# The low parts of the last MLP's weights, made by a transfer that adds

## The chip, the cores and the metric

The kernel runs on one core of one Trainium2 chip. The metric is device time in microseconds for one launch, from the first to the last instruction of the program with what lies around it. Several runs are given with their median.

## The reference

Two transformer blocks on 512 tokens of 1024 features, in float32. The first block has two softmax attentions, gates and an MLP; the second has two layers, each a mixer followed by an MLP with a squared ReLU. Only the last of these MLPs is touched:

```
def _sqrelu_mlp(h, w1, w2):                       # h 512 x 1024, w1 1024 x 4096, w2 4096 x 1024
    return jnp.square(jax.nn.relu(h @ w1)) @ w2

    # second_block, layer 1
    h = _rmsnorm(x, mlp_norm_g[layer])
    x = x + _sqrelu_mlp(h, mlp_w1[layer], mlp_w2[layer])
```

## The kernel before

TensorE takes its operands in a rounded form of float32 (F32R, "fp32r" in the profile). To keep the accuracy of float32, every operand is split into a high part h, the rounded value, and a low part l, the rest: a product is three matmuls, high by high, high by low and low by high, summed in one PSUM bank (`mm3`).

Activations lie with features on partitions, as eight tiles [128, 512 tokens], split into aH and aL. Weights come from DRAM in blocks of [128, 1024], 512 KB each. `load_w` fetches one (tile wraw, four buffers, by SP's queue), ScalarE copies it into the rounded tile wH (three buffers), and VectorE subtracts: wL = wraw - wH (three buffers). In some earlier stages GpSimd does the subtraction (`pool_l`, `lean`); in the layer in question it is VectorE for every block.

`gemm_t_steps` makes one output tile [128, 512] from one block: eight steps of three matmuls, 24 in all. The first `group` tiles of a call go side by side: for each step k the matmuls of tile 0 and tile 1, and those of tile 2 three steps later (`lag`). From then on a tile follows a tile. There are three accumulators in PSUM.

`mlp` goes over the 4096 hidden features in four chunks of 1024. In each chunk the first product makes eight hidden tiles (Relu by ScalarE, times itself by VectorE, split into the pair hd), and the second product takes these through eight blocks of w2; its results are scaled and added to X (`upd`: VectorE multiplies, GpSimd adds, VectorE in the last chunk). That is 64 weight blocks in all. The call of the last layer has `group=3`, which bears on the first chunk only, and its last output tile goes by halves of the tokens, so that its end is short.

The last layer is called at the end of `block_two`, straight after the output product of the odd mixer (`od_out`, eight tiles, line 870), whose results are added to X, squared for the row mean, and split as H by `split_gain` (lines 341 and 342).

The program is laid out by a scheduler at build time, which gives each engine its order from the dependences, the order of the program and its own estimate of when things are ready. At run time every engine, and each queue, works through its instructions in that order.

Of the kernel before, what the change touches and what calls it, by code (L numbers as in the profile page):

```python
# [14 lines left out]
AF = mybir.ActivationFunctionType  # L15
OP = mybir.AluOpType
# [4 lines left out]
P = 128  # L21
# [30 lines left out]
class Weave:  # L52
    """Places small dependent work on TensorE among the steps of long matrix products.

    A task is a generator: it emits one stage, then yields the TensorE time (us, estimated)
    before which its next stage should not stand in TensorE's queue, or a function that
    gives that time, or None while it isn't known."""

# [56 lines left out]
class Build:  # L115
    def __init__(self, nc, tc, ctx, a, out, dbg=None):
        self.nc, self.tc, self.a, self.out, self.dbg = nc, tc, a, out, dbg
        self.ctx = ctx
        self.weave = Weave(self)
        self.lean = False  # L120
        pool = lambda **k: ctx.enter_context(tc.tile_pool(**k))
        self.cn = pool(name="cn", bufs=1)
        self.xp = pool(name="xp", bufs=1)
        self.ap = pool(name="ap", bufs=1)
        self.wp = pool(name="wp", bufs=1)
        self.sm = pool(name="sm", bufs=1)
        self.ps = pool(name="ps", bufs=1, space=PSUM)
        self.dr = pool(name="dr", bufs=1, space=DRAM)
# [49 lines left out]
    def load_w(self, src, n=1024, pools=None, pool_h=False, pool_l=False):  # L178
        nc = self.nc
        (hp, hn, hb), (lp, ln, lb) = pools or ((self.wp, "wH", 3), (self.wp, "wL", 3))  # L180
        r = self.wp.tile([P, 1024], F32, name="wraw", bufs=4)
        nc.sync.dma_start(r[:, :n], src)
        h = hp.tile([P, 1024], F32R, name=hn, bufs=hb)
        if pool_h:
            nc.gpsimd.tensor_scalar(h[:, :n], r[:, :n], 1.0, 0.0, op0=OP.mult, op1=OP.add)
        else:
            nc.scalar.activation(h[:, :n], r[:, :n], AF.Copy)  # L187
        l = lp.tile([P, 1024], F32R, name=ln, bufs=lb)
        (nc.gpsimd if pool_l else nc.vector).tensor_tensor(l[:, :n], r[:, :n], h[:, :n], op=OP.subtract)  # L189
        return h, l  # L190
# [21 lines left out]
    def gemm_t_steps(self, srcs, xs, evac, group=1, kt=KT, pool_l=(), ks=None, halves=False, last=None):  # L212
        """out^T tile m = W[:, 128 m:]^T x^T; srcs: one block [128, kt*128] per tile.

        halves: the first group goes over one half of the tokens first; last: evacuates the
        last tile instead of evac, half by half."""
        m = 0
# [28 lines left out]
    def gemm_n_steps(self, srcs, xs, evac):  # L246
        """out tile [128 tokens, 512] = x W; srcs: four blocks [128, 2 k tiles, 512]."""
        accs = [self.acc() for _ in range(3)] + [self.pg()]
# [24 lines left out]
    def rsqrt(self, out, a, eps):  # L273
        """out = (a + eps) ** -0.5 by Newton steps; small tiles, a may lie in PSUM."""
        nc = self.nc
# [12 lines left out]
    def sumsq(self, src, k, tag="ssq", scale=1.0, apart=False):  # L288
        """adds the squares of tile k (features on partitions) to a running tile, or returns them."""
        nc = self.nc  # L290
        if k == 0:
            s = self.sm.tile([P, NT], F32, name=tag, bufs=1)
            nc.scalar.activation(s, src, AF.Square, scale=scale)
            self.cur[tag] = s
        else:
            q = self.sm.tile([P, NT], F32, name="sq", bufs=2)
            nc.scalar.activation(q, src, AF.Square, scale=scale)
            if apart:
                return q
            nc.vector.tensor_tensor(self.cur[tag], self.cur[tag], q, op=OP.add)  # L300

    def mean_rows(self, *parts, pool=None):
        """mean over features as PSUM [128, 512], the same in every partition."""
        ps = (pool or self.pg)()
# [4 lines left out]
    def rstd_rows(self, ms, name="R"):  # L309
        """(ms + eps) ** -0.5 as SBUF [128, 512]."""  # L310
        nc = self.nc
# [5 lines left out]
    def cols_of(self, R, pool=None):  # L317
        """[128 tokens, 4] columns of rows that are the same in every partition."""
        nc = self.nc
# [7 lines left out]
    def modulate(self, x, k, R, A, shift, hl=None, c=slice(0, NT)):  # L327
        """x R A + shift of tile k, split."""
        nc = self.nc
# [25 lines left out]
def block_one(B):  # L355
    nc, tc, a = B.nc, B.tc, B.a
    with ExitStack() as st:
# [25 lines left out]
        def ada_first(c):  # L383
            """128 columns of shift1 and of scale1, four row tiles at a time side by side on TensorE."""
            pa = B.pmisc()
# [15 lines left out]
        def ada_vec(c):  # L401
            """the same columns on VectorE."""
            row = at.tile([P, 512], F32, name="ada", bufs=2)
# [7 lines left out]
        def ada(part, cb):  # L411
            """512 columns of the modulation, on VectorE."""
            ac = at.tile([P, 512], F32, name="ada", bufs=2)
# [40 lines left out]
        def ev_q(tiles, acc):  # L454
            """1/8 of two heads of 64 rows, each block of 128 queries back to front: for each head
            a tile with the high part in the head's own rows and the low part in the other ones."""
            for b, t in enumerate(tiles):
# [7 lines left out]
        def ev_k(tiles, acc):  # L465
            """for each of two heads a tile with the high part twice; the low parts of both in a third one."""
            for b, t in enumerate(tiles[:2]):
# [67 lines left out]
        def ev_g(m, acc):  # L535
            """sigmoid as exp(-ln(1 + exp(-x)))."""
            t = at.tile([P, NT], F32, name="gt", bufs=4)
# [42 lines left out]
        def ev_last(c, acc):  # L580
            """the last tile of the residual, by halves."""
            t = X[7] if c.start else load_x(7)
# [80 lines left out]
def flip_blocks(t):  # L663
    """columns of [128, 512] with each block of 128 back to front."""
    return bass.AP(tensor=t.tensor, offset=t.offset + P - 1, ap=[t.ap[0], [P, 4], [-1, P]])


def load_strips(B, at):
    """bucket of each distance as one-hot columns with the mask's rows, and the heads' biases."""
    nc, a = B.nc, B.a  # L670
# [7 lines left out]
def bias_strips(B, at, oh):  # L678
    """masked bias by reversed distance, one row per head, in DRAM."""
    nc = B.nc  # L680
# [9 lines left out]
def bias_tile(B, at, h, off, n):  # L690
    """[128 queries, n] additive bias of head h, already masked; the last query first."""
    t = B.strip
# [6 lines left out]
class Attention:  # L699
    """the two softmax attentions of block one, as tasks; heads share buffers, counted in free."""  # L700

# [17 lines left out]
    def head(self, key, h, b, q, k, strip, spans, qk_banks, pt_banks, times, sink=None):  # L719
        """P^T of one head; spans: first and last key of each query tile; banks: tiles that share a PSUM bank."""  # L720
        B, at, W, free = self.B, self.at, self.W, self.free
# [106 lines left out]
def mlp(B, hp, w1, w2, H, upd, group=1, pool_l=(), during=None, mid=None, last=None):  # L828
    """during: called with each step's number in the first product, which goes over half of the tokens first; mid: called after it."""
    nc = B.nc  # L830
# [43 lines left out]
def sq_mlp(B, layer):  # L874
    nc, tc, a, X = B.nc, B.tc, B.a, B.X
    with ExitStack() as st:
# [19 lines left out]
        def end(c, acc):  # L896
            t = hp.tile([P, NT], F32, name="up", bufs=3)[:, c]
            nc.vector.tensor_tensor(t, acc[:, c], R2[:, c], op=OP.mult)
            nc.vector.tensor_tensor(X[7][:, c], X[7][:, c], t, op=OP.add)
            nc.sync.dma_start(B.out[:, 7, c], X[7][:, c])  # L900
        mlp(B, hp, a[f"mlp1_{layer}"], a[f"mlp2_{layer}"], H, upd, group=3, mid=norm, last=end if layer else None)


def even_mixer(B, ev, H):
# [11 lines left out]
    def stats():  # L916
        """rstd of both norms, and the end of the first one."""
        l1 = B.sm.tile([P, NT], F32, name="sq", bufs=2)
# [55 lines left out]
    def gelu(t):  # L974
        """t <- gelu(t), tanh form: t * exp(-ln(1 + exp(-2 u)))."""
        g = ev.tile([P, NT], F32, name="ge", bufs=3)
# [84 lines left out]
    def stick_head(j, b, As):  # L1061
        """A^T of one head, key tiles side by side, masked."""
        need = ("qk", 2 * j), ("qk", 2 * j + 1)
# [26 lines left out]
    def split_y():  # L1090
        """parts of the result take the place of H once that is used up."""
        for k in range(KT):
# [36 lines left out]
def stick_scores(B, ev, q, k, z, h, l, tiles):  # L1129
    """masked scores of some key tiles, and log(1 + exp) of them in two parts."""  # L1130
    nc = B.nc
# [21 lines left out]
def stick_weights(B, z, h, l, tiles):  # L1153
    """z <- exp(z - the sum over this key and the later ones), for some key tiles."""
    nc = B.nc
# [284 lines left out]
```

## Time and profile before

| what | value |
|---|---|
| median of 3 runs | 1937.0 us (1934.53 to 1937.11) |
| span of the profiled execution | 1936.0 us, 1.0 us under the median |
| busy PE / VectorE / ScalarE / GpSimd | 98% / 55% / 40% / 11% of the span |
| DRAM read | 193.86 MB |
| mean DMA rate | 102 GB/s |

The profiled execution is one run; its own time is known by its span. PE is TensorE's matmul queue and PEld its weight loads, which run beside the matmuls; DVE is VectorE, ACT ScalarE, POOL GpSimd, SP the engine that issues the loads. A matmul's shown length contains its pipeline, so that successive matmuls overlap in the rows; the distance from start to start is what counts. Idle time of an engine that is not on the chain which ended last costs nothing.

### The profile page before, as it was taken

How to read it: one execution, taken by the hardware profiler on the slowest of the kernel's cores; microseconds unless marked ns; L12 is line 12 of the kernel's file. 1: busy time of each engine (PE TensorE's matmuls, PEld its weight loads, DVE VectorE, ACT ScalarE, POOL GpSimd, SP SyncE). 2: the span in 40 equal slices, each digit the busy share in tenths (PEclk: the TensorE clock that was granted, in tenths of full speed). 3: DMA queues.
4: the chain of work that ended last, by engine and by line, in shares of the span. 5: the costliest groups of instructions: out<-in, count | busy, mean ns of one | idle time of the engine just before them, and what ended most of it. 6: DMA issues, size and time to landing. Idle time of an engine off the chain costs nothing.

```text
span 1936.0 us, 22136 instructions
## 1 busy us (share of the span) xinstructions
PE 1898.4 (98%) x8570; PEld 1501.6 (78%) x8570; DVE 1066.2 (55%) x1571; ACT 767.3 (40%) x1246; POOL 212.5 (11%) x149
## 2 busy tenths in 40 slices
PE   6999999999999999999899999999999999999999
PEld 3777778888888887776688888888777888888887
DVE  4765668664434346667755445546745554454544
ACT  2455454342323244666634232233436343223231
POOL 1000010010000001325320201100201001210100
PEclk8999999999999999999999999999999999999999
DMA  6523258522223223211122322222231233223221
GB/s 233 165 55 104 89 170 261 188 88 89 97 98 98 89 96 115 66 55 55 44 88 98 98 92 96 96 98 90 89 108 44 77 101 106 97 89 98 98 98 66
DMA packets 61640, 197.43 MB, mean 102 GB/s; under 512 B 6904, under 2 KB 8490, under 8 KB 61536
## 3 DMA queue, kind: packets, MB, share of 16 engines
q1 hardware_dynamic: 57864, 190.34, 29.8%
q10 hardware_dynamic: 3672, 5.69, 1.1%
q8 instruction: 67, 1.10, 0.2%
q14 instruction: 37, 0.30, 0.1%
HBM read 193.86 MB, written 2.15 MB: 101 GB/s over the span
## 4 chain that ended last, share of the span: by engine, by line
PE 88%; DVE 7%; ACT 3%; issue 1%; DMA 1%; SPq 0%; DVEq 0%; ACTq 0%
PE acc L193 79%; PE pm L193 5%; PE pg L193 2%; PE po L193 1%; DVE s L1230 1%; DVE sl L1150 1%; PE pm L196 1%; DMA oh<-ada 1%; ACT wH L187 0%; DVE wL L189 0%; ACT sz L1168 0%; ACT se L1146 0%; ACT se L1147 0%; DVE ge L979 0%; DVE aL L335 0%
## 5 line engine op out<-in xcount | busy, mean ns | idle before, releaser
L187 ACT ACTIVATE wH<-wraw 128x1024 fp32r<-128x1024 f32 (+1 forms) x304 | 314.7, 1037 | 752.3 <-PE acc L193 683.0
L189 DVE TENSOR_TENSOR wL<-wraw,wH 128x1024 fp32r<-128x1024 f32 (+1 forms) x269 | 365.1, 1358 | 298.9 <-ACT wH L187 291.9
L193 PE MATMUL acc<-aH,wH 128*128 128x512 f32 (+1 forms) x1296 | 507.3, 392 | 5.5 <-ACT aH L334 5.0
L193 PE MATMUL acc<-aL,wH 128*128 128x512 f32 (+1 forms) x1296 | 502.2, 387 | 3.4 <-DVE aL L335 3.4
L193 PE MATMUL acc<-aH,wL 128*128 128x512 f32 (+1 forms) x1296 | 501.5, 387 | 0.0
L193 PE MATMUL acc<-hd,wH 128*128 128x512 f32 (+1 forms) x1552 | 483.2, 392 | 0.0
L193 PEld LDWEIGHTS acc<-hd,wH 128*128 128x128 f32 x1552 | 289.4, 187 | 70.8 <-issue 1.0
L193 PE MATMUL acc<-hd,wL 128*128 128x512 f32 (+1 forms) x776 | 304.0, 392 | 0.0
L193 PEld LDWEIGHTS acc<-aH,wH 128*128 128x128 f32 x1296 | 244.2, 189 | 62.7 <-issue 9.2
L193 PEld LDWEIGHTS acc<-aL,wH 128*128 128x128 f32 x1296 | 244.4, 189 | 53.8 <-DVE aL L335 4.3
L193 PEld LDWEIGHTS acc<-aH,wL 128*128 128x128 f32 x1296 | 244.4, 189 | 50.7 <-issue 1.2
L193 PEld LDWEIGHTS acc<-hd,wL 128*128 128x128 f32 x776 | 145.2, 187 | 35.2
L189 POOL TENSOR_TENSOR wL<-wraw,wH 128x1024 fp32r<-128x1024 f32 x38 | 96.2, 2536 | 675.7 <-ACT wH L187 654.7
L889 POOL TENSOR_TENSOR X<-X,up 128x512 f32<-128x512 f32 x48 | 69.9, 1456 | 573.2 <-DVE up L887 322.0
L887 DVE TENSOR_TENSOR up<-acc,R 128x512 f32<-128x512 f32 x63 | 43.6, 692 | 153.7 <-PE acc L193 153.7
L270 ACT ACTIVATE hd<-rl 128x512 fp32r<-128x512 f32 x96 | 60.6, 632 | 120.5 <-DVE rl L837 120.4
L271 DVE TENSOR_TENSOR hd<-rl,hd 128x512 fp32r<-128x512 f32 x96 | 66.3, 692 | 60.8 <-ACT hd L270 60.8
L655 DVE SCALAR_TENSOR_TENSOR X<-acc,mod,X 128x512 f32<-128x512 f32 x32 | 24.0, 751 | 88.9 <-PE acc L193 88.9
L193 PE MATMUL acc<-s,wH 128*128 128x512 f32 (+1 forms) x208 | 66.6, 379 | 0.0
L837 DVE TENSOR_TENSOR rl<-rl,acc 128x512 f32<-128x512 f32 x96 | 65.1, 681 | 0.0
L193 PE MATMUL pm<-s,s 64*128 64x384 f32 (+7 forms) x160 | 55.7, 436 | 0.0
L836 ACT ACTIVATE rl<-acc 128x512 f32<-128x512 f32 x96 | 55.4, 580 | 0.0
(312 smaller groups left out, 1917.6 us busy)
## 6 DMA issues: line engine op xcount, KB each, us to landing
wraw<-mlp SPq DMA_DIRECT2D x128, 512.0 KB, 3.2
wraw<-w SPq DMA_DIRECT2D x64, 512.0 KB, 3.2
wraw<-ada SPq DMA_DIRECT2D x32, 512.0 KB, 4.5
wraw<-w_in SPq DMA_DIRECT2D x30, 512.0 KB, 3.5
oh<-ada SPq DMA_DIRECT2D x32, 256.0 KB, 4.8
wraw<-od_in SPq DMA_DIRECT2D x16, 512.0 KB, 3.3
wraw<-ev_in SPq DMA_DIRECT2D x12, 512.0 KB, 3.3
X<-x SPq DMA_DIRECT2D x16, 256.0 KB, 4.6
```

What stands on the lines that cost most here:

```text
L187: nc.scalar.activation(h[:, :n], r[:, :n], AF.Copy)
L189: (nc.gpsimd if pool_l else nc.vector).tensor_tensor(l[:, :n], r[:, :n], h[:, :n], op=OP.subtract)
L193: self.weave.placed(self.nc.tensor.matmul(out, w, x, start=start, stop=stop), out, x)
L196: self.weave.placed(self.nc.tensor.transpose(out, x, self.ident[:x.shape[0], :x.shape[0]]), out, x)
L270: nc.scalar.activation(hl[0], src, AF.Copy)
L271: nc.vector.tensor_tensor(hl[1], src, hl[0], op=OP.subtract)
L655: nc.vector.scalar_tensor_tensor(X[m], acc, mod[:, 40 + m:41 + m], X[m], op0=OP.mult, op1=OP.add)
L836: nc.scalar.activation(r, acc, AF.Relu)
L837: nc.vector.tensor_tensor(r, r, acc, op=OP.mult)
L887: nc.vector.tensor_tensor(t, acc, R2, op=OP.mult)
L889: eng.tensor_tensor(X[m], X[m], t, op=OP.add)
L1150: nc.vector.tensor_tensor(l[:, c], e[:, :w], h[:, c], op=OP.subtract)
```

## The change

For the last layer only, `load_w` no longer subtracts on VectorE. ScalarE makes a second copy of the raw block into the tile wL, with scale -1, so that wL holds the negated high part, and GpSimd's queue issues a transfer of the same block of weights from DRAM which adds what it reads to what lies in wL. The raw block itself is still loaded, copied to wH, and read once more for the negated copy. The other lines of the diff take texts out of functions and are not shown.

```
@@ class Build, __init__
         self.lean = False
+        self.low_by_dma = False
@@ load_w
         l = lp.tile([P, 1024], F32R, name=ln, bufs=lb)
+        if self.low_by_dma:
+            nc.scalar.activation(l[:, :n], r[:, :n], AF.Copy, scale=-1.0)
+            nc.gpsimd.dma_start(l[:, :n], src, accum_op=OP.add)
+            return h, l
         (nc.gpsimd if pool_l else nc.vector).tensor_tensor(l[:, :n], r[:, :n], h[:, :n], op=OP.subtract)
         return h, l
@@ sq_mlp
+        B.low_by_dma = layer == 1
         mlp(B, hp, a[f"mlp1_{layer}"], a[f"mlp2_{layer}"], H, upd, group=3, mid=norm, last=end if layer else None)
```

## Rows read from the trace of the kernel before

**Rows 1.** Head of the page, and its busy time by engine.
```profile
span 1936.0 us, 22136 instructions
...
PE 1898.4 (98%) x8570; PEld 1501.6 (78%) x8570; DVE 1066.2 (55%) x1571; ACT 767.3 (40%) x1246; POOL 212.5 (11%) x149
```

**Rows 2.** The chain that ended last: start, length, engine, tile and line.
```profile
1497.60 124.39 PE acc L193 x543
1621.99 0.86 PE pg L193 x2
1622.85 309.67 PE acc L193 x1368
```

**Rows 3.** Busy time by stretch, the layer: PE, PEld, DVE, ACT, POOL, clock, DMA.
```profile
1578.30:1936.00 357.70, 354.21 (x1563) 289.25 (x1561) 166.20 (x171) 103.51 (x130) 37.02 (x24) 1.00 0.28 92
```

**Rows 4.** Timeline of ScalarE, first product: start, length, [idle before, releaser].
```profile
1860.52 1.06 ACT L187 ACTIVATE wH<-wraw 128x1024 fp32r<-128x1024 f32 x1 [1.86 <-PE acc L193]
1861.48 0.58 ACT L836 ACTIVATE rl<-acc 128x512 f32<-128x512 f32 x1
...
1865.96 1.06 ACT L187 ACTIVATE wH<-wraw 128x1024 fp32r<-128x1024 f32 x1 [1.86 <-PE acc L193]
```

**Rows 5.** Timeline of VectorE in the same tile.
```profile
1861.61 1.23 DVE L189 TENSOR_TENSOR wL<-wraw,wH 128x1024 fp32r<-128x1024 f32 x1 [2.23 <-ACT wH L187]
```

**Rows 6.** Timeline of PE where the layer's fourth tile begins.
```profile
1594.63 0.39 PE L193 MATMUL acc<-aH,wH 128*128 128x512 f32 x1
...
1595.08 0.39 PE L193 MATMUL acc<-aH,wL 128*128 128x512 f32 x1
```

**Rows 7.** Timeline of ScalarE, second product, the last two blocks.
```profile
1910.06 1.06 ACT L187 ACTIVATE wH<-wraw 128x1024 fp32r<-128x1024 f32 x1 [4.49 <-PE acc L193]
1915.66 1.06 ACT L187 ACTIVATE wH<-wraw 128x1024 fp32r<-128x1024 f32 x1 [4.54 <-PE acc L193]
```

**Rows 8.** Costliest groups of the page, GpSimd: busy, mean ns | idle before.
```profile
L189 POOL TENSOR_TENSOR wL<-wraw,wH 128x1024 fp32r<-128x1024 f32 x38 | 96.2, 2536 | 675.7 <-ACT wH L187 654.7
L889 POOL TENSOR_TENSOR X<-X,up 128x512 f32<-128x512 f32 x48 | 69.9, 1456 | 573.2 <-DVE up L887 322.0
```

**Rows 9.** The tile wraw from 1590 on: issues (ns), and landing times.
```profile
L182 SPq DMA_DIRECT2D wraw<-mlp x57: 327/328/328, 1593.5 to 1896.1; - x57
...
DMA to landing us min/median/max: 3.1/3.2/3.8
```

**Rows 10.** DMA queues, 1550 to 1936: packets, MB, share of 16 engines.
```profile
q1 hardware_dynamic: 10656, 36.18, 28.1%
```

**Rows 11.** DMA issues, whole span: KB each, median us to landing.
```profile
oh<-ada SPq DMA_DIRECT2D x32, 256.0 KB, 4.8
```

**Rows 12.** Timeline of ScalarE at the start of the layer.
```profile
1572.65 1.06 ACT L187 ACTIVATE wH<-wraw 128x1024 fp32r<-128x1024 f32 x1 [3.34 <-PE acc L193]
...
1574.21 0.71 ACT L341 ACTIVATE aH<-X,vecs 128x512 fp32r<-128x512 f32 x1
1578.26 1.06 ACT L187 ACTIVATE wH<-wraw 128x1024 fp32r<-128x1024 f32 x1 [3.34 <-PE acc L193]
...
1591.20 1.06 ACT L187 ACTIVATE wH<-wraw 128x1024 fp32r<-128x1024 f32 x1 [10.68 <-PE acc L193]
1592.17 1.06 ACT L836 ACTIVATE rl<-acc 128x512 f32<-128x512 f32 x2
```

**Rows 13.** Timeline of PE: the layer's first matmul.
```profile
1578.29 0.40 PE L193 MATMUL acc<-aH,wH 128*128 128x512 f32 x1
```

**Rows 14.** Timeline of PE near the kernel's start.
```profile
20.94 0.70 PE L193 MATMUL acc<-aH,wH 128*128 128x512 f32 x2 [2.16 <-ACT aH L334]
...
22.13 0.80 PE L193 MATMUL acc<-aH,wH 128*128 128x512 f32 x1
23.81 0.80 PE L193 MATMUL acc<-aL,wH 128*128 128x512 f32 x1 [0.88 <-DVE aL L335]
...
25.53 0.80 PE L193 MATMUL acc<-aH,wL 128*128 128x512 f32 x1
```

More of the change, by code (lines that the diff above doesn't have):

```diff
@@ L120, in __init__ @@
         self.lean = False
+        self.low_by_dma = False
         pool = lambda **k: ctx.enter_context(tc.tile_pool(**k))
@@ L188, in load_w @@
         l = lp.tile([P, 1024], F32R, name=ln, bufs=lb)
+        if self.low_by_dma:
+            nc.scalar.activation(l[:, :n], r[:, :n], AF.Copy, scale=-1.0)
+            nc.gpsimd.dma_start(l[:, :n], src, accum_op=OP.add)
+            return h, l
         (nc.gpsimd if pool_l else nc.vector).tensor_tensor(l[:, :n], r[:, :n], h[:, :n], op=OP.subtract)
@@ L900, in end @@
             nc.sync.dma_start(B.out[:, 7, c], X[7][:, c])
+        B.low_by_dma = layer == 1
         mlp(B, hp, a[f"mlp1_{layer}"], a[f"mlp2_{layer}"], H, upd, group=3, mid=norm, last=end if layer else None)
```

## The prediction

> **What bounds the kernel now.** I read the page's head first: the span is 1936.0 us and PE is busy 98% of it [rows 1]. The three timed runs have a median of 1937.0 us, so the profiled execution stands 1.0 us under it, and my sum is made on the span and then carried to the median. I then looked up where the changed layer lies. In the chain that ended last, its whole stretch is two unbroken PE pieces: 543 matmuls from 1497.60, the row mean at 1621.99, and 1368 matmuls from 1622.85 to 1932.5 [rows 2]. The table by stretch says the same for the layer itself (1578.3 to the end): PE busy 354 of 357.7 us at full granted clock (2.4 GHz), VectorE busy only 166, ScalarE 104, GpSimd 37, the DMA engines 28% [rows 3]. So the layer is PE from end to end. What the change takes off VectorE is not on the path, and it can only lose time, by making a low part late.
>
> How late may a low part come? A weight slot frees when its tile's last product is done, and ScalarE's copy to wH starts on that release; two such copies are 5.44 us apart [rows 4], which is one tile of 24 matmuls. VectorE's subtraction follows and ends 2.3 us after the copy began [rows 5]. There are three slots, so the tile that gets the slot starts two tiles later, 10.9 us, and its first low product is the third matmul, 0.45 us further on [rows 6]: needed at 11.3 us, ready at 2.3, so 9 us of slack today. In the second product of a chunk a tile takes 5.60 us [rows 7] and the slack is slightly larger.
>
> **The change, part by part.**
>
> *Removed:* 64 subtractions of 1.23 us [rows 5], 79 us of VectorE's 166. Worth 0: PE hides all of them, as the 9 us show. A gain would need PE to wait for VectorE here, and it doesn't.
>
> *Added on ScalarE:* 64 copies with scale -1. The row for the same shape is 1.06 us [rows 4], so 68 us on an engine busy 104 of 358. Cover: ScalarE idles in every tile. In its queue the Relu stands right behind the wH copy today [rows 4]; it belongs to an earlier part of the program, so I expect wH, Relu, negated copy. VectorE's multiply then no longer stands behind the subtraction, and the hd pair is ready no later than now. If the negated copy came ahead of the Relu, hd would be about half a us later at each of the four chunk boundaries: 0 to 2 us together, taken as 0.
>
> *Added on GpSimd's queue:* 64 transfers, each issued when the negated copy is done: 1.06 + 0.58 + 1.06 = 2.7 us after the release. That leaves 11.3 - 2.7 = 8.6 us to issue and land. Behind a waiting transfer in that queue stand the 24 additions to X (1.5 us each [rows 8]); only the next chunk's addition to the same X waits for one, over 80 us away: nothing. An addition that stands ahead of one costs it at most its own 1.5 us, which leaves 7.1.
>
> *The transfer itself.* No accumulating transfer is in the trace of before. A plain load of this size lands 3.2 us after issue [rows 9]. The load queue used 28.1% of 386 us for 36.18 MB in the last stretch [rows 10], so one load of 0.524 MB takes 108.5/69 = 1.57 us of the sixteen engines' time, and 1.6 us of the 3.2 is fixed. The accumulating one must fetch two operands, the weights from DRAM and the negated copy from SBUF: I count 2 x 1.57 = 3.1. It starts together with the plain load of the tile four further on, which is freed by the same negated copy and shares the engines: 3.1 + 1.57 = 4.7, plus 1.6 fixed, plus the issue. For the issue SP's row is 0.33 us [rows 9] and GpSimd's slowest row of this tile size, its own subtraction, 2.5 us [rows 8]; I take 0.33, since it is the row of a DMA issue. Sum 6.6 us against 8.6: hidden, with 2 us to spare (nothing to spare with the 2.5). Bounds: one operand's cost gives 5.0; the slowest row in the list, 4.8 us for 256 KB [rows 11], would give 19 us for two operands of 512 KB.
>
> The Trainium skill ("Collectives: The Full Stack", section "The bandwidth ceiling: the fold count and why AG ≠ RS ≠ AR") also counts an addition in the DMA as two source reads and puts nothing on the arithmetic. No row here shows it; by it the engine time is my 3.1 us. Another page speaks against the change: "DMA: Bandwidth & Descriptors", table "Specifications", gives a transfer issued by GpSimd about 1 us to its first byte, against 0.6 from SP; no run here has one, and by it the sum would be an estimated 7.0 us, still hidden.
>
> *The loads:* wraw is now freed by the negated copy (2.7 us) instead of the subtraction (2.3 us), so SP's next load goes out 0.4 us later. It is needed four tiles, 22 us, further on: 0. Engine time per tile rises from 1.57 to 4.7 of about 5.5 us, 85%.
>
> *The start of the layer* is where there is less room, because the first three tiles run side by side. The second one's slot was freed 5.6 us before the layer began: its wH copy is at 1572.65, then a square and an aH copy follow in ScalarE's queue [rows 12]; with the negated copy behind them it ends at 1576.0, and 6.6 us later is 1582.6. PE starts at 1578.29 [rows 13], and the sixth matmul, at 1579.4, is that tile's first low product: 3.2 us late. The third tile's copy is at 1578.26: its low part lands at 1588.2 against a use at 1584.2 (the 27th matmul), 4.0 late in all. The fourth tile's slot frees at 1591.20 and two Relus follow [rows 12]: it lands at 1600.9 against 1595.1 [rows 6], another 5.8. In the order of today that is 9.8 us. But PE's queue is laid out by expected readiness, not only by the order written: near the kernel's start three aH products stand together ahead of the aL and wL ones, although the code writes aH, aL, wL for one tile before the next [rows 14]. So PE can be given the first tile's 24 matmuls (5.4 us) ahead, which covers 3.2 and 4.0 and frees that slot some 7 us earlier, which covers 5.8. Bounds 0 and 9.8; near 0 by that row, and I take 2 us for a low part that lands later than the layout expects.
>
> *The end* stays: the last transfer is issued near 1917.8, two copies after 1915.66 [rows 7], lands near 1924.4, and is first used near 1927 (the last tile begins 5.6 us before 1932.5).
>
> Sum: 0 + 0 + 0 + 2 = +2 us. 1937 + 2 = 1939.
>
> **The rivals.** A difference within 0.2%, 3.9 us, can't be told from no change with this measurement.
>
> A (forecast): hidden, start costs 0 to 3.9 us. For it: 9 us of slack and idle ScalarE and GpSimd. Chance 0.52, own range 1935 to 1941.
>
> B: hidden in the long run, but the start is laid out as today or the layout misjudges the landing: 4 to 16 us (9.8 at my 6.6 us, twice as much more for each us of latency). 1941 to 1953. Against it: rows 14. Chance 0.15.
>
> C: slower, because the sixteen DMA engines become the bound. It decides where the accumulating transfer takes more than 5.5 - 1.57 = 3.9 us of engine time, 2.5 times a plain load. At three times a tile takes 6.3 us, +0.8 x 62 tiles = 50 us: 1987; at four times 7.85, +146: 2083. The same sign comes from latency alone: beyond 8.6 us every further us costs half a us per tile, 31 us. For it: engines already 85% filled by my count and no row for the operation. Against: each of its parts is an ordinary transfer. Chance 0.28.
>
> D: faster by more than 3.9 us. The place would be PE matmuls that run closer together than their 0.227 us [rows 6] once the subtractions are gone; no row ties that spacing to VectorE. Chance 0.05.
>
> **How the numbers follow.** The time is A's. Faster is D, 0.05; same is A, 0.52; slower is B and C, 0.43. The range takes in A, B and C up to about three and a half times a plain load's engine time: 1934 to 2030, leaving out some 0.15.
>
> **What would show it.** In the profile after: VectorE's wL rows of the layer gone; twice the ScalarE copies, still about 1.06 us; 64 transfers on a GpSimd queue landing within 8.6 us; PE still one piece from 1623 on; at most a few us of PE waiting for the transfers between 1578 and 1600. Landings over 8.6 us, or a tile period over 5.6 us with the DMA engines near full, would mean C and a wrong prediction. A wait of 4 us or more at the start only would mean B.

## The result and the profile after

The changed kernel takes 1950.55 us (median of 4 runs, 1947.8 to 1953.85) against 1937.05 us before (4 runs): the medians are 13.5 us apart, a quotient of 1.0070. The ratio on record, which is an estimate over all runs and not that quotient, is 1.0063, with a 95% interval of 1.0043 to 1.0083. Single runs scatter: over all of them the kernel before took 1933.5 to 1942.8 us, with a mean granted clock of about 0.994 near 1936 and 0.991 near 1941. The result is inside the forecast range and inside rival B's own (1941 to 1953); the likeliest case, A, did not come.

The profiled execution of after has a span of 1946.0 us. Its last layer begins at 1574.16, 4.1 us earlier than in the profile of before [rows 13], so the spans can't be compared straight. The layer itself can. The table by stretch, from the layer's first matmul to its last (columns as in [rows 3]):

```profile
1574.16:1942.46 368.30, 358.42 (x1563) 291.43 (x1561) 73.10 (x107) 158.60 (x192) 84.40 (x86) 0.99 0.83 178
```

By the same cut the layer of before is 354.22 us, all of it PE:

```profile
1578.29:1932.51 354.22, 354.22 (x1563) 289.26 (x1561) 165.35 (x169) 103.52 (x130) 37.02 (x24) 1.00 0.28 92
```

The layer has grown by 14.1 us, which covers the 13.5 us of the result. VectorE fell from 165 to 73 us, ScalarE rose from 104 to 159, the DMA engines from 28% to 83%. PE is now short of the stretch by 9.9 us, and its waits in the layer are these (waited for; us in total, times, longest):

```profile
PE acc L198 <- DMA wL<-mlp: 9.9, 3, 5.8
```

All of PE's waiting is for the new transfers, three times. The timeline of PE shows where. The first wait is for the layer's second block, at the sixth matmul:

```profile
1574.16 0.40 PE L198 MATMUL acc<-aH,wH 128*128 128x512 f32 x1
...
1575.08 0.39 PE L198 MATMUL acc<-aL,wH 128*128 128x512 f32 x1
1579.03 0.50 PE L198 MATMUL acc<-aH,wL 128*128 128x512 f32 x1 [3.56 <-DMA wL<-mlp]
...
1580.62 0.63 PE L198 MATMUL acc<-aL,wH 128*128 128x512 f32 x1
1581.05 0.63 PE L198 MATMUL acc<-aH,wL 128*128 128x512 f32 x1
...
1596.40 1.02 PE L198 MATMUL pg<-ssq,colD 128*128 128x512 f32 x2
1597.02 0.63 PE L198 MATMUL acc<-aH,wH 128*128 128x512 f32 x1
1597.49 0.40 PE L198 MATMUL acc<-aL,wH 128*128 128x512 f32 x1
1603.68 0.80 PE L198 MATMUL acc<-aH,wL 128*128 128x512 f32 x1 [5.79 <-DMA wL<-mlp]
...
1715.80 0.51 PE L198 MATMUL acc<-aH,wL 128*128 128x512 f32 x1 [0.52 <-DMA wL<-mlp]
```

The second wait is for the fourth block, and the third is a single near miss far on in the layer. From the matmul ahead of each wait to the one behind it, less the usual 0.227 us, PE lost 3.72, 5.96 and 0.68 us: 10.4 together. Behind the first wait the matmuls stand 0.43 us apart instead of 0.23. The table by stretch around the two waits gives the granted clock (last column but two):

```profile
1579.03:1579.83 0.80, 0.80 (x3) 0.68 (x4) 0.00 (x0) 0.00 (x0) 0.00 (x0) 1.00 1.08 149
1579.83:1583.20 3.37, 3.37 (x10) 2.59 (x9) 0.00 (x0) 0.00 (x0) 0.00 (x0) 0.51 0.73 146
1583.20:1597.00 13.80, 13.80 (x61) 11.13 (x59) 1.98 (x3) 4.48 (x7) 0.86 (x1) 1.00 0.04 11
1597.60:1603.68 6.08, 0.29 (x2) 0.00 (x1) 1.90 (x3) 4.93 (x7) 1.73 (x2) 0.73 0.94 214
1603.68:1607.30 3.62, 3.62 (x9) 2.88 (x10) 0.00 (x0) 0.00 (x0) 0.00 (x0) 0.51 1.05 261
```

After each of the two long waits PE works some 3.5 us at 0.51 of full clock, the 1.2 GHz level, which costs 1.7 us each (1579.03 to 1583.47 holds 12 matmul steps: 4.44 - 12 x 0.227). Together that is 10.4 + 3.4 = 13.8 of the 14.1 us.

The transfers themselves, in the view of the tile wL (issue durations in ns; time to landing in us) and of the DMA queues from 1550 on (q0 is GpSimd's, q1 SP's):

```profile
L192 POOL DMA_DIRECT2D wL<-mlp x64: 862/865/1013, 1565.3 to 1928.0; - x64
...
DMA to landing us min/median/max: 5.2/7.7/9.7
```
```profile
q0 software_dynamic: 9216, 33.56, 49.9%
q1 hardware_dynamic: 10392, 35.20, 30.3%
```

A transfer takes 49.9% of 396 us over 64 = 3.09 us of the sixteen engines, twice the 1.57 of a plain load [rows 10]. (The plain loads beside it take 30.3% of 396 us over 67 = 1.79 us each, so a part of the 3.09 may be crowding.) It lands 7.7 us after GpSimd begins to issue it, of which the issue is 0.87. The loads beside it now land after 6.2 us (median, in the view of the tile wraw) instead of 3.2 [rows 9]; PE waits for none of them.

### The profile page after: what moved, and what is told of

It is laid out like the page before. It is cut to its first block, busy times and chain, and to the rows that moved or that the text cites. A ratio compares the mean times of both kernels' runs of the same rounds, so it can differ in the third digit from the quotient of the medians.

```text
span 1946.0 us, 22224 instructions
## 1 busy us (share of the span) xinstructions
PE 1899.8 (98%) x8570; PEld 1503.7 (77%) x8570; DVE 972.6 (50%) x1507; ACT 824.5 (42%) x1310; POOL 261.8 (13%) x213
## 4 chain that ended last, share of the span: by engine, by line
PE 87%; DVE 6%; issue 3%; ACT 2%; DMA 2%; SPq 0%; POOL 0%; DVEq 0%; ACTq 0%; POOLq 0%
PE acc L198 76%; PE pm L198 6%; PE pg L198 2%; PE po L198 2%; DMA wL<-mlp 1%; DVE s L1236 1%; DMA oh<-ada 1%; PE pm L201 1%; DVE wL L194 0%; ACT wH L188 0%; DVE sl L1156 0%; DVE ssq L305 0%; DVE ge L985 0%; DVE ge L986 0%; ACT ge L988 0%
## 5 line engine op out<-in xcount | busy, mean ns | idle before, releaser
L194 DVE TENSOR_TENSOR wL<-wraw,wH 128x1024 fp32r<-128x1024 f32 (+1 forms) x205 | 267.6, 1306 | 216.9 <-ACT wH L188 212.3
L894 POOL TENSOR_TENSOR X<-X,up 128x512 f32<-128x512 f32 x48 | 63.7, 1328 | 329.3 <-DVE up L892 248.2
L192 POOL DMA_DIRECT2D wL<-mlp x64 | 55.8, 872 | 281.1 <-ACT wL L191 280.9
L191 ACT ACTIVATE wL<-wraw 128x1024 fp32r<-128x1024 f32 x64 | 67.0, 1047 | 0.0
```

Source lines behind the costliest of these rows:

```text
L191: nc.scalar.activation(l[:, :n], r[:, :n], AF.Copy, scale=-1.0)
L192: nc.gpsimd.dma_start(l[:, :n], src, accum_op=OP.add)
L894: eng.tensor_tensor(X[m], X[m], t, op=OP.add)
```

## The experiments

The theory is that the loss sits only at the layer's start, where three tiles go side by side and a low part has less room than the transfer needs, and that from there on the transfer is hidden. Its rivals are a price per block (traffic, the second copy), a fixed price of the new queue, and a transfer that is too slow wherever it stands. For each run the table gives the ratio on record, and the layer in its profile from the first matmul to the end of the last. The ratios go by the runs of before beside each kernel: their median was 1937.5 us (26 runs) for the four kernels that follow after in the table, and 1940.91 us (29 runs) for the other ones. Ahead of the layer the same code runs in all of them, but the layer began at 1574 to 1584 us in these profiles, so the layer's own length is the finer measure.

| kernel | ratio to before (95%) | layer, us | PE waits for transfers, us |
|---|---|---|---|
| before | 1 | 354.2 | none |
| after | 1.0063 (1.0043 to 1.0083) | 368.3 | 3.6, 5.8, 0.5 |
| first six blocks on VectorE | 1.0005 (0.9994 to 1.0017) | 354.3 | none |
| first four on VectorE | 1.0026 (1.0014 to 1.0038) | 358.9 | 2.1, 0.2 |
| only the first six by transfer | 1.0084 (1.0070 to 1.0098) | 366.8 | 3.6, 4.3 |
| one tile after the other | 1.0014 (1.0004 to 1.0024) | 354.5 | none |
| the same, again | 1.0004 (0.9994 to 1.0014) | 354.8 | none |
| control: VectorE, one after the other | 0.9995 (0.9985 to 1.0005) | 354.2 | none |
| transfer without adding, one after the other | 0.9994 (0.9983 to 1.0005) | 354.2 | none |

**First six blocks on VectorE.**

```
-        if self.low_by_dma:
+        self.nlow += self.low_by_dma
+        if self.low_by_dma and self.nlow > 6:
```

> The first six weight blocks of the last layer get their low parts on VectorE as before, the other 58 from the adding transfer. Theory (the loss sits in two waits at the layer's start, 3.7 and 6.0 us, with some 3 us of half clock behind them; the rest is hidden): no wait at the start, time that of the kernel before, 1936 to 1939 us, from 0 to 1 us over it. Rival 1 (doubled DMA traffic or the second ScalarE copy costs a little in every block): 58/64 of the 13.5 us stay, 1949 us. Rival 2 (a fixed price for having the queue at all): 1950 us.

This kernel took 1938.79 us against 1937.5, ratio 1.0005. The row of the layer, with 58 of the 64 transfers still in it:

```profile
1577.83:1932.09 354.26, 354.25 (x1563) 289.31 (x1561) 77.48 (x111) 154.99 (x188) 80.92 (x82) 1.00 0.83 178
```

PE is busy throughout, with the DMA engines at 83% as in after. So neither the traffic, nor ScalarE's second copy, nor the queue costs anything that can be seen, and rivals 1 and 2 fall.

**First four on VectorE** (`> 4` in the same line).

> As the run before, but only the first four blocks on VectorE. Theory, if only the blocks that waited in the trace matter (the second and the fourth): 1937 us. Theory, if the fifth block was merely covered by the fourth one's wait (its slot frees with the second block's end, 9.3 us before its first use by today's order, and its transfer lands some 14 us after that): a new wait of 3 to 5 us plus half clock, 1941 to 1944 us. Rival (cost spread over all blocks): 1949 us.

This kernel took 1942.46 us, ratio 1.0026. The fifth block now waits; the timeline of PE:

```profile
1602.02 0.39 PE L200 MATMUL acc<-aL,wH 128*128 128x512 f32 x1
1604.53 0.80 PE L200 MATMUL acc<-aH,wL 128*128 128x512 f32 x1 [2.12 <-DMA wL<-mlp]
1605.12 0.63 PE L200 MATMUL acc<-aH,wH 128*128 128x512 f32 x1
```

The wait is shorter than the expected 3 to 5 us, but it is there: in after, the fourth block's wait covered the fifth one's. A wait that is taken away uncovers the next.

**Only the first six by transfer** (`<= 6`).

> Only the first six blocks by the adding transfer, 58 on VectorE. Theory: nearly the whole loss with a tenth of the transfers, 1947 to 1951 us (waits of about 3.7 and 6 us in the same two places). Rival (cost spread over all blocks): 6/64 of 13.5, 1938 us.

This kernel took 1954.26 us, ratio 1.0084. The row of the layer, and the two waits in the timeline of PE:

```profile
1577.16:1943.91 366.75, 358.81 (x1563) 291.89 (x1561) 167.50 (x165) 107.00 (x134) 34.20 (x28) 0.99 0.31 96
```
```profile
1582.06 0.50 PE L200 MATMUL acc<-aH,wL 128*128 128x512 f32 x1 [3.59 <-DMA wL<-mlp]
...
1605.28 0.80 PE L200 MATMUL acc<-aH,wL 128*128 128x512 f32 x1 [4.34 <-DMA wL<-mlp]
```

A tenth of the transfers costs the layer 12.5 of the 14.1 us, in the same two places. The time lies above what I expected and 4 us above that of after, though the layer in the profile is 1.5 us shorter than there. The two intervals overlap; the profile is of the shortest of the six runs (1949.26 us), no trace of the others was kept, and what the 4 us are stays open.

**One tile after the other.**

```
-        mlp(B, hp, ..., H, upd, group=3, mid=norm, ...)
+        mlp(B, hp, ..., H, upd, group=1 if layer else 3, mid=norm, ...)
```

> All 64 blocks by the adding transfer, but the last layer's first three tiles go one after the other instead of side by side, so that the second block is needed 5.4 us later and its slot and the following ones free one by one. Theory (the room at the start is what lacks): no wait over 1 us at the start, 1937 to 1939 us. Rival (the transfer is too slow or too late however the tiles stand): still 1947 to 1951 us.

This kernel took 1941.11 us, ratio 1.0014, which is 2 us above the range that I gave. PE has no wait for a transfer, and the layer is 354.5 us. The transfer did not change (view of wL from 1574 on); only the room did:

```profile
DMA to landing us min/median/max: 5.3/7.7/8.6
```

The 0.14% over before is not in the layer, so I ran it again beside a control, the kernel before with the same `group=1`. (The expectation counts the layer to the start of its last matmul, the table to its end, 0.28 us later.)

> The kernel with one tile after the other and all low parts by transfer, once more, beside its own control (next run). In its first profile the layer itself took 354.2 us from first to last matmul, as before (353.9), while the whole was 0.14% over the kernel before. Theory (nothing is left in the layer, the 0.14% is scatter of the start of the kernel): within 0.1% of the control and 1936 to 1940 us. Rival (the transfers or the queue cost 2 to 3 us outside the layer): 2 to 3 us over the control again.

> The control: the kernel before (low parts on VectorE) with the last layer's first three tiles one after the other. Expected 1936 to 1939 us, no change, since PE has no wait in the layer either way. If it is 2 to 3 us slower than the kernel before, the order of the tiles and not the transfer made the 0.14%.

The two took 1941.42 and 1939.99 us, ratios 1.0004 and 0.9995 to the runs of before beside them; both times lie 1 us or more above my ranges, but so does the 1940.91 of before. The table by stretch of the layer, transfers first, control second (each in its own profile):

```profile
1578.14:1932.96 354.82, 354.82 (x1563) 288.95 (x1561) 73.36 (x107) 158.78 (x192) 84.32 (x86) 1.00 0.88 185
```
```profile
1576.21:1930.43 354.22, 354.22 (x1563) 289.26 (x1561) 165.72 (x169) 103.89 (x130) 37.06 (x24) 1.00 0.28 92
```

Of the 1.4 us between them 0.6 is in the layer, and their intervals overlap, so a price of a us outside the layer is neither shown nor excluded. 92 us of VectorE's time more or less make no difference that can be seen. Since PE is full in the layer of before, I see no version of this edit that would beat it; none was tried beyond these.

**Both squared-ReLU layers.**

```
-        B.low_by_dma = layer == 1
+        B.low_by_dma = True
```

> Low parts by the adding transfer in both squared-ReLU layers (128 blocks). Theory (waits at the start of a layer): the first of the two layers also begins with three tiles side by side behind a product of eight tiles, so it has waits in the same two places, 10 us with 3 us of half clock, and nothing later: 1961 to 1967 us. Rival (a fixed price for having the queue): 1950 us. Rival (cost per block): also about 1964 us, but spread over the layer in the trace.

This kernel took 1992.31 us, ratio 1.0271 (1.0251 to 1.0292), far over what I expected, and for a reason in my edit: nothing takes the switch back, so the odd mixer between the two layers took its low parts by transfer too, 160 blocks in all. The waits of PE from 960 on, by what it waited for:

```profile
PE acc L198 <- DMA wL<-mlp: 17.8, 4, 6.2
PE acc L198 <- DMA wL<-od_in: 10.7, 2, 7.2
PE acc L198 <- DMA wL<-od_out: 8.0, 2, 5.1
```

Four products begin with three tiles side by side, and each has exactly two waits; 32 blocks of the odd mixer and 128 of the layers give eight waits, not 160. The waits are 36.5 of the 51 us. The rest is about what the half clock costs: behind each of the eight waits the timeline of PE has slow matmuls at a granted clock of 0.50 or 0.51, worth 1.6 to 2.8 us, 15.6 together. The four waits of the odd mixer with their slow matmuls come to some 26 us; without them the time would be an estimated 1966 us, inside the range that I gave. So the theory held, and the forecast that I drew from it left out the odd mixer.

**A transfer that doesn't add.**

```
-            nc.gpsimd.dma_start(l[:, :n], src, accum_op=OP.add)
+            nc.gpsimd.dma_start(l[:, :n], src)
```

> One tile after the other as above, but GpSimd's transfer does not add: it overwrites wL with the weights (so the low parts are not the low parts; this part of the computation is changed). It reads one operand instead of two. My count (engine time goes by operands read, 1.57 us each): engine time 1.5 to 1.7 us per transfer instead of 3.1, landing 1.5 to 2.5 us earlier than 7.7 us. Rival (what makes it slow is GpSimd's queue, not the adding): still 3 us and 7 us or more. Time 1936 to 1940 us in both.

This run also has one tile after the other, and its wL holds the weights themselves, so the kernel leaves out the low parts. It took 1937.86 us, ratio 0.9994. The DMA queues from 1585 to 1935, and the view of wL:

```profile
q0 software_dynamic: 8928, 32.51, 25.8%
```
```profile
L192 POOL DMA_DIRECT2D wL<-mlp x55: 527/530/570, 1624.3 to 1923.1; - x55
...
DMA to landing us min/median/max: 3.7/4.7/6.4
```

25.8% of 350 us over 62 transfers is 1.46 us each, half of 3.09. So the engine time goes by the operands read, and the adding also costs 0.33 us more of issue. Without it a transfer lands after 4.7 us and not 7.7: 3.0 us earlier, more than I expected. How much of the 3.0 us comes from the lighter traffic beside it is not separated.

## Why the prediction came out as it did

The range (1934 to 2030) held the time, but it was wide: the likeliest case A (0.52) was wrong, and B (0.15) came, by the sign set for it, waits of PE at the start with one of over 4 us. By steps:

- *Removed from VectorE, worth 0:* right. The control and the two runs with one tile after the other differ by 92 us of VectorE and by 0.2 to 0.6 us in the layer. (I had counted 79 us for the 64 subtractions; those in the layer of before average 1.55 us, not the 1.23 of [rows 5].)
- *ScalarE, 64 copies:* right in size (1.05 us each). The order at the start was other than I took it: the negated copy went straight behind the wH copy, ahead of the square and aH. The second block's transfer went out 2.3 us after its wH copy began, where I had reckoned 3.3: 1.0 us earlier.
- *The transfer:* the engine time was right (3.1 counted, 3.09 measured), and so were the two operands. The landing was 7.7 us against my 6.6; 0.5 of the difference is the issue, which takes GpSimd 0.87 us and not SP's 0.33, the rest is not separated. The Trainium skill ("DMA: Bandwidth & Descriptors", section "Specifications") has a GpSimd transfer's first byte about 0.4 us later than SP's (its table has about 1 us against 0.6). By it the sum had been an estimated 7.0 us, nearer and still short; no run here shows the first byte by itself. The Trainium skill's account of an addition as two source reads ("Collectives: The Full Stack", section "The bandwidth ceiling: the fold count and why AG ≠ RS ≠ AR") agrees with the two runs: 3.09 against 1.46 us, 2.1 times. (The bound of 19 us came from a row of 4.8 us that is not the slowest of its list, where one of 256 KB has 5.6; nothing hung on it.)
- *Hidden in the long run, 8.6 us of room:* right. In after one block of some sixty missed it. The chain that ended last shows that one (start, length):

```profile
1706.59 9.17 DMA wL<-mlp
```

It landed 9.17 us after its issue and PE waited 0.52 for it, so its room was 8.65 us. With a median of 7.7 little was to spare; case C did not come.

- *The start:* this step failed. "In the order of today" I had worked out 4.0 and 5.8 us, and then I set them to 2, because PE's queue had been laid out by readiness near the kernel's start [rows 14]. Here it kept today's order, and PE lost 3.72 and 5.96 us. The layer's first 74 matmuls have the same order of operands in after and in before, and only the row mean was drawn forward, from 1621.83 to 1596.40. The names of the operands are the same for every tile, but the sixth matmul waited until the second block's transfer landed, 8.1 us after its issue, so PE was not given the first tile's 24 matmuls ahead:

```profile
1570.84 0.86 POOL L192 DMA_DIRECT2D wL<-mlp  x1 [4.57 <-ACT wL L191]
...
1595.79 0.86 POOL L192 DMA_DIRECT2D wL<-mlp  x1 [18.51 <-ACT wL L191]
```

That 3.72 and 5.96 come so near to 4.0 and 5.8 is in part luck. Of the 4.0 I had put 3.2 on the second block and 0.8 on the third: the second went out 1.0 us earlier and landed 1.5 us later than I reckoned, and the third had no wait, since the second's wait and the slow matmuls behind it held PE back. The fourth (the issue at 1595.79) landed after 7.8 us, 1.2 later than reckoned, and was first needed 1.3 us later, 5.2 us after its wH copy began and not 3.9. What [rows 14] show is PE going on with other tiles' high products, beside low parts of activations that were late; that the same would hold for late weights was a guess. Why the scheduler left the order as it was stays open; that it expected the transfers to land in time would fit, and is only argued.
- *Not in the sum at all:* the half clock after the two waits, 3.4 us. With it and the near miss, rival B in my own numbers (9.8) comes to 13.9 against 14.1 measured in the layer, with the luck that is told above.

The first run shows that without the start no loss is left that can be seen, the third that the start alone suffices, and the one with one tile after the other that room is what lacked: the same transfer, landing after 7.7 us, is hidden there. A faster transfer with three tiles side by side was not tried. The second run shows that it isn't enough to spare the two blocks that waited: four were too few, six are enough, and five were not tried.

## What to carry to other kernels

An operation that is hidden in the steady state must be checked once more where a product begins: with tiles side by side a buffer frees later and is needed earlier, and there a longer latency shows in full. Where the written order gives a wait and the scheduler is hoped to take it away, put the written order's number into the forecast, and add what the clock takes after each wait (1.6 to 2.8 us in these runs, behind waits of 2.1 us and more). And moving work off an engine that nobody waits for has nothing to gain by itself, whatever that engine's share of busy time.

## What the runs showed of the hardware that I had not expected

- An adding transfer of 512 KB takes 3.09 us of the sixteen engines against 1.46 without the adding, and GpSimd 0.87 us against 0.53 to issue; nothing in PE's pace changes beside it (PE's 1563 matmuls take 354.2 to 354.8 us with the DMA engines at 28%, 83%, 87% or 88%, where PE does not wait for a transfer).
- After waits of 3.6 and 5.8 us PE's granted clock was 0.51 for some 3.5 us, and after the 2.1 us wait of the second experiment 0.50 for some 3.4 us. After the first of these it fell only 0.8 us after PE had gone on; after the 0.5 us wait no slow matmul followed.
